# Hi and lo parts of each prepared weight stored in turn, element by element, in an encoder kernel on one core

## The chip, the core and the metric

The kernel runs on one core of one Trainium2 chip. The time is device time in microseconds, from one launch. Every change is judged against the kernel before; here smaller is better. Times of several executions are given as their median.

## The reference

Two layers of a bidirectional encoder over 256 tokens of 1024 channels, all in float32. What matters here is that nearly all the work is products with weights:

```
for i in range(2):
    h = x + 0.5 * swiglu(rms_norm(x, norm_ffn1[i]), w_ffn1_in[i], w_ffn1_out[i])     # 1024 -> 2 x 2816 -> 1024
    u = rms_norm(h, norm_mix[i])
    q, k, v, c, g = split(u @ w_in[i])                                               # 512, 128, 128, 1024, 2048
    y_attn = window_attention(norm(q), norm(k), v, sink[i], rel_bias) @ w_attn_out[i]
    y_conv = silu(layer_norm(depthwise_conv(glu(c)))) @ w_conv_out[i]
    h = h + (sigmoid(g)[:, :1024] * y_attn + sigmoid(g)[:, 1024:] * y_conv) @ w_o[i]
    h = h + 0.5 * swiglu(rms_norm(h, norm_ffn2[i]), w_ffn2_in[i], w_ffn2_out[i])
    x = h + (p[i] @ w_pe_proj[i]) * sigmoid(rms_norm(h, norm_pe[i]) @ w_pe_gate[i])
```

## The kernel before

**Products in three matmuls.** A float32 weight is cut into two parts of the type float32r: `hi`, the weight rounded to that type, and `lo`, what is left over. Activations are cut the same way. A product is then hi·hi + hi·lo + lo·hi, which `mm3` (lines 309 to 317) issues as three matmuls for each of the 128-row pieces of the contraction. In `mm3` the weight is the stationary operand (128 columns, loaded into TensorE's array by a load of its own ahead of each matmul) and the activations, 256 tokens, are the moving operand. Two stages do it the other way round: keys and values (`half`, lines 669 to 678) and queries (`part`, lines 713 to 722) have the activations as the stationary and the weights as the moving operand. `w_attn_out` and `w_conv_out` are used as plain float32 straight from the loaded buffer (line 852).

**Weights as one long list.** `Weights` holds a list of units (transfers of up to 1 MB from memory into one of 4 `raw` buffers, issued on SyncE's queue, line 76) and a list of specs (what one `get` hands out: k pieces of n columns). `get` (line 124) prepares LOOK = 6 specs ahead of the one that it hands out. `prep_upto` (line 80) prepares one: ScalarE copies the raw weight into `w_hi` with rounding (line 100), then VectorE writes raw minus hi into `w_lo` (line 101). The pool `w_pool` has 7 buffers of `w_hi` and 7 of `w_lo`, 4 KB in each partition, so that a copy into a buffer waits for the last matmul of the spec seven places earlier.

**Stages and order.** For each layer: 22 steps of `gate_up` (tiles `ps_gu`), 8 of `down` (`ps_fo`), the mixer (`ps_c` convolution input, `ps_kv`, `ps_q`, `ps_g` gates, attention between them, `ps_ao`, `ps_co`, then `ps_wo`), the second feed-forward part, and the per-layer embedding (`ps_pp`, `ps_pe`). TensorE runs in the program's order. The order on the other engines comes from a planner that works with priorities; `ws.later` hooks put attention steps between the weight products by hand. The convolution's taps run on VectorE in the background of the mixer (line 612).

**Where tiles lie.** Small tiles that nothing reads (`edge` of 96 bytes, `gap0`, `gap1` of 64) stand between the pools. In the program as built, every prepared weight tile starts at a multiple of 128 bytes in its partition and every activation tile that `mm3` reads starts 64 bytes after one.

Of the kernel before, what the change touches and what calls it, by code (L numbers as in the profile page):

```python
# [10 lines left out]
F32R = mybir.dt.float32r  # L11
# [4 lines left out]
P = 128  # L16
T = 256
D = 1024
KD = D // P
# [4 lines left out]
QD = 512  # L24
CD = 512
KC = CD // P
# [15 lines left out]
class Weights:  # L42
# [13 lines left out]
        self.units.append((k, n, sources))  # L56
        return len(self.units) - 1

    def spec(self, k, n, pieces):

        self.specs.append((k, n, pieces, False))

    def raw_spec(self, unit, k, c0, n):
        self.specs.append((k, n, [(unit, 0, c0, 0, n)], True))

    def limit(self):
        held = [p[0] for s in self.specs[self.next_get : self.next_prep] if s[3] for p in s[2]]
        return min(held) + RAW_BUFS - 1 if held else len(self.units) - 1

    def load_upto(self, u):  # L70
# [9 lines left out]
    def prep_upto(self, i):  # L80
        nc = self.nc
        while self.next_prep <= min(i, len(self.specs) - 1):
            k, n, pieces, as_is = self.specs[self.next_prep]
            for u, *_ in pieces:
                self.load_upto(u + RAW_BUFS - 2)
                if u >= self.next_load:
                    return
            if as_is:
                ((u, k0, s0, _, w),) = pieces
                self.ready[self.next_prep] = self.raw[u][:, k0 : k0 + k, s0 : s0 + w]  # L90
                self.next_prep += 1
                continue
            hi = self.w_pool.tile([P, KD * P], F32R, name="w_hi")
            lo = self.w_pool.tile([P, KD * P], F32R, name="w_lo")
            hv = hi[:, : k * n].rearrange("p (k n) -> p k n", n=n)
            lv = lo[:, : k * n].rearrange("p (k n) -> p k n", n=n)
            for u, k0, s0, d0, w in pieces:
                src = self.raw[u][:, k0 : k0 + k, s0 : s0 + w]
                parts = (
                    nc.scalar.copy(out=hv[:, :, d0 : d0 + w], in_=src),  # L100
                    nc.vector.tensor_tensor(  # L101
                        out=lv[:, :, d0 : d0 + w],
                        in0=src,
                        in1=hv[:, :, d0 : d0 + w].bitcast(F32),
                        op=ALU.subtract,
                    ),
                )
                if self.pin:
                    for ins in parts:
                        self.pin(ins)  # L110
                    self.pin = None
            self.ready[self.next_prep] = (hv, lv)
            self.next_prep += 1
# [25 lines left out]
def encoder_kernel(ctx: ExitStack, tc: tile.TileContext, a: dict, out: bass.AP):  # L139
# [30 lines left out]
    for i in range(4):  # L170
        s = slice(i * 256, (i + 1) * 256)
# [32 lines left out]
    ws = Weights(tc, raw_pool, w_pool)  # L204
# [4 lines left out]
    def cols_unit(w, k, c0, n):  # L209
        return ws.unit(k, n, [(whole, w[: k * P, c0 : c0 + n].rearrange("(k p) n -> p k n", p=P))])  # L210
# [25 lines left out]
    def mix_specs(l):  # L236
        w = a["w_in"][l]
        c0 = QD + 2 * P

        def conv_specs(j, n):  # L240
            uv = cols_unit(w, KD, c0 + j * P, n * P)
            ug = cols_unit(w, KD, c0 + CD + j * P, n * P)
            for c in range(n):
                ws.spec(KD, P, [(uv, 0, c * P, 0, P)])
                ws.spec(KD, P, [(ug, 0, c * P, 0, P)])

        conv_specs(0, 2)
        ukv = cols_unit(w, KD, QD, 256)
        for i in range(2):
            ws.spec(KC, 256, [(ukv, i * KC, 0, 0, 256)])  # L250
        for i in range(2):
            uq = cols_unit(w[i * KC * P : (i + 1) * KC * P], KC, 0, QD)
            for k in range(0, KC, 2):
                ws.spec(2, QD, [(uq, k, 0, 0, QD)])
        conv_specs(2, 2)
        g0 = QD + 2 * P + 2 * CD
        for j in range(8):
            u = cols_unit(w, KD, g0 + j * 256, 256)
            for c in range(2):
                ws.spec(KD, P, [(u, 0, c * P, 0, P)])  # L260
        w = a["w_attn_out"][l]
        for j in range(2):
            src = w[:, j * 512 : (j + 1) * 512].rearrange("(v c p) n -> v p c n", v=2, p=HD)
            u = ws.unit(KC, 512, [
                (lambda v: v[0:HD], src[0]),
                (lambda v: v[HD : 2 * HD], src[1]),
            ])
            for c in range(2):
                ws.raw_spec(u, KC, c * 256, 256)
        w = a["w_conv_out"][l]  # L270
        for j in range(2):
            u = cols_unit(w, KC, j * 512, 512)
            for c in range(2):
                ws.raw_spec(u, KC, c * 256, 256)
        w = a["w_o"][l]
        for j in range(4):
            u = cols_unit(w, KD, j * 256, 256)
            for c in range(2):
                ws.spec(KD, P, [(u, 0, c * P, 0, P)])
# [10 lines left out]
    for l in range(L):  # L290
        ffn_specs(a["w_ffn1_in"][l], a["w_ffn1_out"][l], quick=l == 0)
        mix_specs(l)
        ffn_specs(a["w_ffn2_in"][l], a["w_ffn2_out"][l])
        pe_specs(l)
# [797 lines left out]
```

## Time and profile before

| what | value |
|---|---|
| time, median of 3 executions | 1156.94 us (1156.45 to 1158.47) |
| profiled execution: span, first to last instruction | 1155.8 us |
| TensorE busy with matmuls (PE) | 1136.7 us, 98% |
| TensorE busy with loads of the stationary operand (PEld) | 1100.9 us, 95% |
| VectorE (DVE) | 812.1 us, 70% |
| ScalarE (ACT) | 610.4 us, 53% |
| read from memory | 200.53 MB, mean 174 GB/s over the span |

The span is the only time that the profiled execution has; it lies 1.1 us under the median of the executions without a profile. PE and PEld are two rows of one engine: the load for the next matmul runs while the present one streams, so both can be busy all the time. The matmuls' recorded durations overlap (each ends after the next has begun), so the pace of TensorE is read from the starts of successive matmuls, not from durations.

### The profile page before, as it was taken

What the parts mean: (1) busy time and instruction counts of PE and PEld (TensorE: products, weight loads), DVE (VectorE), ACT (ScalarE), POOL (GpSimd) and SP (SyncE); (2) the same over time, 40 slices, a digit from 0 to 9 for tenths busy, and PEclk for the clock granted to TensorE, in tenths of its full rate; (3) what the DMA queues carried; (4) which work ended last, traced back from release to release, by engine and by line L of the source; (5) the groups of instructions that cost most, each with busy time, mean ns of one, the idle gap of its engine ahead of it and who ended that gap; (6) DMA issues with size and microseconds to landing.
All of it is one profiled execution on the core that took longest, in us unless ns stands there. A gap on an engine that the chain in (4) does not pass through costs nothing.

```text
span 1155.8 us, 21813 instructions
## 1 busy us (share of the span) xinstructions
PE 1136.7 (98%) x9082; PEld 1100.9 (95%) x9082; DVE 812.1 (70%) x1214; ACT 610.4 (53%) x1029; POOL 88.8 (8%) x123
## 2 busy tenths in 40 slices
PE   7999999999989999999999999999999999999998
PEld 7999999998879999999999999999987899999997
DVE  5866656798767766656886666669986686666564
ACT  6644444676346544444664444457753564444443
POOL 3000001211002000001110000113000010000110
PEclk9999999999999999999999999999999999999999
DMA  8866556545074565546556464566522664644541
GB/s 256 265 236 213 170 176 208 182 149 138 8 254 157 187 215 168 179 166 219 188 177 204 162 207 156 171 218 197 143 77 65 227 228 152 214 163 149 200 147 37
DMA packets 195695, 203.00 MB, mean 176 GB/s; under 512 B 3731, under 2 KB 188899, under 8 KB 195596
## 3 DMA queue, kind: packets, MB, share of 16 engines
q1 hardware_dynamic: 195564, 201.60, 52.9%
q8 instruction: 71, 1.16, 0.4%
q14 instruction: 28, 0.23, 0.1%
q10 hardware_dynamic: 32, 0.01, 0.0%
HBM read 200.53 MB, written 1.06 MB: 174 GB/s over the span
## 4 chain that ended last, share of the span: by engine, by line
PE 95%; DMA 2%; DVE 2%; ACT 1%; issue 0%; SPq 0%; ACTq 0%; DVEq 0%
PE ps_gu L317 14%; PE ps_gu L315 14%; PE ps_gu L316 14%; PE ps_fo L315 7%; PE ps_fo L317 7%; PE ps_fo L316 7%; PE ps_g L315 3%; PE ps_g L317 3%; PE ps_g L316 3%; PE ps_ao L852 2%; DMA raw<-in_w_o_dram 2%; PE ps_s L760 1%; PE ps_wo L316 1%; PE ps_c L315 1%; PE ps_pe L317 1%; PE ps_c L317 1%
## 5 line engine op out<-in xcount | busy, mean ns | idle before, releaser
L101 DVE TENSOR_TENSOR w_lo<-raw,w_hi 128x1024 fp32r<-128x1024 f32 (+1 forms) x368 | 441.6, 1204 | 227.8 <-ACT w_hi L100 225.9
L100 ACT CAST w_hi<-raw 128x1024 fp32r<-128x1024 f32 (+1 forms) x368 | 377.8, 1032 | 411.6 <-PE ps_gu L316 207.5
L315 PE MATMUL ps_fo<-h_hi,w_hi 128*128 128x256 f32 x704 | 196.1, 279 | 0.0
L316 PE MATMUL ps_fo<-h_lo,w_hi 128*128 128x256 f32 x704 | 195.9, 279 | 0.0
L317 PE MATMUL ps_fo<-h_hi,w_lo 128*128 128x256 f32 x704 | 195.9, 279 | 0.0
L317 PEld LDWEIGHTS ps_fo<-h_hi,w_lo 128*128 128x128 f32 x704 | 131.8, 188 | 0.0
L315 PEld LDWEIGHTS ps_fo<-h_hi,w_hi 128*128 128x128 f32 x704 | 131.8, 188 | 0.0
L316 PEld LDWEIGHTS ps_fo<-h_lo,w_hi 128*128 128x128 f32 x704 | 131.7, 187 | 0.0
L404 POOL TENSOR_TENSOR sq_acc<-sq_acc,sq 128x256 f32<-128x256 f32 x56 | 56.9, 1015 | 887.0 <-ACT sq L403 886.5
L315 PE MATMUL ps_gu<-x0h,w_hi 128*128 128x256 f32 x352 | 99.4, 282 | 2.0 <-ACT x L460 2.0
L612 DVE SCALAR_TENSOR_TENSOR y<-cpad,cw,y 128x256 f32<-128x256 f32 x240 | 101.2, 477 | 0.1
L317 PE MATMUL ps_gu<-x0h,w_lo 128*128 128x256 f32 x352 | 99.4, 282 | 0.2 <-DVE w_lo L101 0.2
L316 PE MATMUL ps_gu<-x0l,w_hi 128*128 128x256 f32 x352 | 98.9, 281 | 0.0
L315 PE MATMUL ps_gu<-xf0h,w_hi 128*128 128x256 f32 x352 | 98.6, 280 | 0.0
L315 PE MATMUL ps_gu<-xf1h,w_hi 128*128 128x256 f32 x352 | 98.6, 280 | 0.0
L316 PE MATMUL ps_gu<-xn0l,w_hi 128*128 128x256 f32 x352 | 98.5, 280 | 0.0
L315 PE MATMUL ps_gu<-xn0h,w_hi 128*128 128x256 f32 x352 | 98.4, 280 | 0.0
L316 PE MATMUL ps_gu<-xf0l,w_hi 128*128 128x256 f32 x352 | 98.4, 280 | 0.0
L316 PE MATMUL ps_gu<-xf1l,w_hi 128*128 128x256 f32 x352 | 98.4, 280 | 0.0
L317 PE MATMUL ps_gu<-xf0h,w_lo 128*128 128x256 f32 x352 | 98.3, 279 | 0.0
L317 PE MATMUL ps_gu<-xf1h,w_lo 128*128 128x256 f32 x352 | 98.3, 279 | 0.0
L317 PE MATMUL ps_gu<-xn0h,w_lo 128*128 128x256 f32 x352 | 98.2, 279 | 0.0
(225 smaller groups left out, 2677.8 us busy)
## 6 DMA issues: line engine op xcount, KB each, us to landing
raw<-in_w_ffn_in_dram SPq DMA_DIRECT2D x86, 1024.0 KB
raw<-in_w_in_dram SPq DMA_DIRECT2D x30, 1024.0 KB
raw<-in_w_ffn_out_dram SPq DMA_DIRECT2D x32, 896.0 KB
raw<-in_w_ffn_out_dram SPq DMA_DIRECT2D x16, 1024.0 KB
raw<-in_w_o_dram SPq DMA_DIRECT2D x8, 1024.0 KB
raw<-in_w_pe_gate_dram SPq DMA_DIRECT2D x8, 1024.0 KB
raw<-in_w_attn_out_dram SPq DMA_DIRECT2D x8, 512.0 KB
raw<-in_w_conv_out_dram SPq DMA_DIRECT2D x4, 1024.0 KB
```

The lines of the kernel that those rows point to most:

```text
L100: nc.scalar.copy(out=hv[:, :, d0 : d0 + w], in_=src),
L101: nc.vector.tensor_tensor(out=lv[:, :, d0 : d0 + w], in0=src, in1=hv[:, :, d0 : d0 + w].bitcast(F32), op=ALU.subtract,),
L315: nc.tensor.matmul(ps, wh[:, k0 + k, cols], xh[:, kx, :], start=f, stop=False)
L316: nc.tensor.matmul(ps, wh[:, k0 + k, cols], xl[:, kx, :], start=False, stop=False)
L317: nc.tensor.matmul(ps, wl[:, k0 + k, cols], xh[:, kx, :], start=False, stop=e)
L404: nc.gpsimd.tensor_tensor(out=self.acc, in0=self.acc, in1=sq, op=ALU.add)
L612: nc.vector.scalar_tensor_tensor(out=y[:, i, :], in0=src, scalar=w, in1=y[:, i, :], op0=ALU.mult, op1=ALU.add)
L760: nc.tensor.matmul(ps[:, c, :], qT[v * HD : (v + 1) * HD, c, qb * P : (qb + 1) * P], kT[v * HD : (v + 1) * HD, :], start=True, stop=True,)
L852: nc.tensor.matmul(ps[:, c * T : (c + 1) * T], w[:, k, c * P : (c + 1) * P], x[:, k, :], start=k == 0, stop=k == KC - 1,)
```

## The change

Hi and lo of a spec now share one tile `w` of twice the size. Where the weight will be the stationary operand, element 2j of a row holds hi and element 2j + 1 holds lo, so each is read and written with a step of two elements. Where it will be the moving operand (keys and values, queries), the spec is marked `moving`, and hi and lo keep two halves of the tile, each without gaps. Numbers of instructions and of transfers, the arithmetic and the buffers' total size stay the same.

```diff
-    def spec(self, k, n, pieces):
-        self.specs.append((k, n, pieces, False))
+    def spec(self, k, n, pieces, moving=False):
+        self.specs.append((k, n, pieces, "moving" if moving else "stationary"))
...
-            hi = self.w_pool.tile([P, KD * P], F32R, name="w_hi")
-            lo = self.w_pool.tile([P, KD * P], F32R, name="w_lo")
-            hv = hi[:, : k * n].rearrange("p (k n) -> p k n", n=n)
-            lv = lo[:, : k * n].rearrange("p (k n) -> p k n", n=n)
+            w = self.w_pool.tile([P, 2 * KD * P], F32R, name="w")
+            if kind == "moving":
+                hv, lv = (w[:, i * KD * P :][:, : k * n].rearrange("p (k n) -> p k n", n=n) for i in range(2))
+            else:
+                both = w[:, : 2 * k * n].rearrange("p (k n s) -> p k n s", n=n, s=2)
+                hv, lv = both[:, :, :, 0], both[:, :, :, 1]
...
-            ws.spec(KC, 256, [(ukv, i * KC, 0, 0, 256)])
+            ws.spec(KC, 256, [(ukv, i * KC, 0, 0, 256)], moving=True)
...
-                ws.spec(2, QD, [(uq, k, 0, 0, QD)])
+                ws.spec(2, QD, [(uq, k, 0, 0, QD)], moving=True)
```

More of the change, by code (lines that the diff above doesn't have):

```diff
@@ L57, in unit @@
         return len(self.units) - 1
-    def spec(self, k, n, pieces):
-        self.specs.append((k, n, pieces, False))
+    def spec(self, k, n, pieces, moving=False):
+        self.specs.append((k, n, pieces, "moving" if moving else "stationary"))
     def raw_spec(self, unit, k, c0, n):
-        self.specs.append((k, n, [(unit, 0, c0, 0, n)], True))
+        self.specs.append((k, n, [(unit, 0, c0, 0, n)], "raw"))
     def limit(self):
-        held = [p[0] for s in self.specs[self.next_get : self.next_prep] if s[3] for p in s[2]]
+        held = [p[0] for s in self.specs[self.next_get : self.next_prep] if s[3] == "raw" for p in s[2]]
         return min(held) + RAW_BUFS - 1 if held else len(self.units) - 1
@@ L82, in prep_upto @@
         while self.next_prep <= min(i, len(self.specs) - 1):
-            k, n, pieces, as_is = self.specs[self.next_prep]
+            k, n, pieces, kind = self.specs[self.next_prep]
             for u, *_ in pieces:
@@ L87, in prep_upto @@
                     return
-            if as_is:
+            if kind == "raw":
                 ((u, k0, s0, _, w),) = pieces
```

## The prediction

> **What bounds the kernel now.** I read the page's engine rows and its chain first, then the stretches of the span, and then the starts of single matmuls. The page:
>
> ```profile
> span 1155.8 us, 21813 instructions
> ...
> PE 1136.7 (98%) x9082; PEld 1100.9 (95%) x9082; DVE 812.1 (70%) x1214; ACT 610.4 (53%) x1029; POOL 88.8 (8%) x123
> ...
> PE 95%; DMA 2%; DVE 2%; ACT 1%; issue 0%; SPq 0%; ACTq 0%; DVEq 0%
> ```
>
> TensorE is 95% of the chain that ends last. The waits say that it hardly ever waits for a prepared weight: the only such row is the first below, once in the run, while ScalarE waits for the matmuls to free its buffers (second row), so preparation runs a full seven buffers ahead.
>
> ```profile
> PE ps_gu L317 <- DVE w_lo L101: 0.2, 1, 0.2
> ACT w_hi L100 <- PE ps_gu L316: 207.5, 141, 1.9
> ```
>
> So the time is the number of matmuls times their pace. A long stretch of the second feed-forward part (columns: stretch, its length, then busy time and count of PE, PEld, DVE, ACT):
>
> ```profile
> 385.00:580.00 195.00, 195.00 (x1656) 194.95 (x1656) 132.09 (x172) 99.31 (x147) 10.14 (x11) 1.00 0.56 187
> ```
>
> 195.00 / 1656 = 0.1178 us per matmul of 256 moving columns. Is that the least it can be? The order of time, start and duration first:
>
> ```profile
> 13.77 0.41 PE L315 MATMUL ps_gu<-x0h,w_hi 128*128 128x256 f32 x1
> ...
> 14.62 0.41 PE L316 MATMUL ps_gu<-x0l,w_hi 128*128 128x256 f32 x1
> ...
> 214.01 0.28 PE L676 MATMUL ps_kv<-w_hi,xm0h 128*128 128x256 f32 x1
> ...
> 219.35 0.28 PE L678 MATMUL ps_kv<-w_hi,xm0l 128*128 128x256 f32 x1
> 219.69 0.40 PE L721 MATMUL ps_q<-w_lo,xm0h 128*128 128x512 f32 x1
> ...
> 226.00 0.39 PE L721 MATMUL ps_q<-w_lo,xm0h 128*128 128x512 f32 x1
> ...
> 312.63 0.60 PE L874 MATMUL ps_yt<-ident,y 128*128 128x128 f32 x4
> 313.06 0.60 PE L852 MATMUL ps_ao<-o,raw 128*128 128x256 f32 x2
> ```
>
> Keys and values have the same sizes, 48 matmuls with 256 moving columns and a load of 128, but weight and activations exchanged: (219.35 - 214.01) / 47 = 0.1136. Transposes, each with a load of 128 columns, follow one another every (313.06 - 312.63) / 4 = 0.1075. So 0.1178 holds about 0.010 us that is neither streaming nor loading at its best. It is constant through the run and does not depend on what the other engines do, so I take it to arise inside TensorE's own reads: the load for the next matmul and the moving stream read SBUF at once, and 0.1136 against 0.1178 shows that which operand is read on which side matters.
>
> **The change, part by part.**
>
> *The stationary operand read with a step of two.* A matmul streams 256 x 4 = 1024 bytes of each partition while the load beside it runs over 128 x 4 = 512. After the change the load runs over 128 x 8 = 1024 bytes in the same time: both streams walk through the addresses at the same speed, and by the layout they start 64 bytes apart modulo 128. If they disturb each other where they meet, then today one overtakes the other again and again; at equal speed they stay apart. No row shows a stationary operand with a step, so the price has two ends from rows: 0.1136 (keys and values, the other fp32r rows of this size) and 0.1075 (the transposes' row). Neither row is nearer in kind: the first has the same types, the second shows what a load and a short stream need at least. I take the middle, 0.1106, a gain of 0.0072 for each matmul. How many there are:
>
> ```profile
> L315 PE MATMUL ps_fo<-h_hi,w_hi 128*128 128x256 f32 x704 | 196.1, 279 | 0.0
> L315 PE MATMUL ps_gu<-x0h,w_hi 128*128 128x256 f32 x352 | 99.4, 282 | 2.0 <-ACT x L460 2.0
> L315 PE MATMUL ps_g<-xm0h,w_hi 128*128 128x256 f32 x128 | 36.8, 287 | 0.0
> L315 PE MATMUL ps_pe<-xe_h,w_hi 128*128 128x256 f32 x128 | 36.5, 286 | 0.0
> L315 PE MATMUL ps_wo<-ym_h,w_hi 128*128 128x256 f32 x128 | 35.1, 282 | 0.5 <-ACT ym_h L448 0.5
> L315 PE MATMUL ps_c<-xm1h,w_hi 128*128 128x256 f32 x64 | 18.1, 282 | 0.0
> L315 PE MATMUL ps_pp<-pT_h,w_hi 128*128 128x256 f32 x32 | 8.9, 280 | 0.0
> ```
>
> Three lines each: 3 x 704, 12 x 352 (four feed-forward parts), 6 x 128 (two layers), 3 x 128, 3 x 128, 6 x 64, 3 x 32, together 8352. Some 17 at the start run at (14.62 - 13.77) / 4 = 0.2125 and gain nothing. 8335 x 0.0072 = 60.0 us less. Ends: 8335 x 0.0042 = 35 and 8335 x 0.0103 = 86.
>
> The Trainium skill, SBUF — State Buffer, section Specifications (TRN2), gives lines of 16 bytes of which at least two accesses must hit each for full bandwidth. By it a step of two 4-byte elements, two hits in a line, is just allowed, and the load would not get longer; no run here shows it yet. The skill's TensorE: Matmul & The Clock Gate, section "Step-by-step: what each phase is for", speaks against my gain: two independent read ports, and a load that takes no bandwidth from the running matmul. By that the sum would be 1156; the 0.1136 beside 0.1178 does not fit it well, and I weigh it as the first rival.
>
> *Writing hi and lo with a step.*
>
> ```profile
> L101 DVE TENSOR_TENSOR w_lo<-raw,w_hi 128x1024 fp32r<-128x1024 f32 (+1 forms) x368 | 441.6, 1204 | 227.8 <-ACT w_hi L100 225.9
> L100 ACT CAST w_hi<-raw 128x1024 fp32r<-128x1024 f32 (+1 forms) x368 | 377.8, 1032 | 411.6 <-PE ps_gu L316 207.5
> ```
>
> Of 368 each, 12 (keys, values, queries) keep their form. A copy and a subtraction take 1.03 and 1.20 us for a tile whose 24 matmuls last 24 x 0.1106 = 2.65 us, so nothing shows on the path unless a row grows: the cover is 2.65 - 1.20 = 1.45 us less what else VectorE does in that time. Bounds: nothing, or twice as long. I take nothing: both rows go at 1.0 to 1.2 ns for each of 1024 elements, and no row shows a cost of a gap. Twice as long would bring VectorE to 812 + 441.6 x 356 / 368 = 1239 us busy, over the span; it is a rival below.
>
> *One tile for both parts.* If a reader of hi now also waits for the writer of lo, the first product waits; elsewhere preparation is ahead. The first matmul starts at 11.12 and the first with lo at 12.11:
>
> ```profile
> 11.12 0.58 PE L315 MATMUL ps_gu<-x0h,w_hi 128*128 128x256 f32 x1 [2.04 <-ACT x L460]
> ...
> 12.11 0.58 PE L317 MATMUL ps_gu<-x0h,w_lo 128*128 128x256 f32 x1 [0.19 <-DVE w_lo L101]
> ```
>
> Between 0 and 0.99 us; I take the two matmuls that would move behind it, 2 x 0.2125 = 0.4. A buffer becomes free one matmul later (line 317, not 316), 0.12 us out of a lead of seven tiles: nothing. Queues and transfers are unchanged, on SyncE's queue too.
>
> *What is late next.* Faster products need weights faster: the stretch above read 187 GB/s, times 0.1178 / 0.1106 is 199, and the page's second slice has 265:
>
> ```profile
> GB/s 256 265 236 213 170 176 208 182 149 138 8 254 157 187 215 168 179 166 219 188 177 204 162 207 156 171 218 197 143 77 65 227 228 152 214 163 149 200 147 37
> ```
>
> In the mixer VectorE's taps must finish before the layer norm; there 3 x 64 + 3 x 128 = 576 products arrive 576 x 0.0072 = 4.1 us sooner per layer, and VectorE waits there for products long enough to follow: 12.7 us in two layers for the gates alone.
>
> ```profile
> DVE g L833 <- PE ps_g L317: 12.7, 8, 2.3
> ```
>
> *Sum:* 1155.8 - 60.0 + 0.4 = 1096.2 us of span. The median lies 1.1 above the span, so 1097 us.
>
> **The rivals.**
>
> *The pace stays.* Queries speak for it: (226.00 - 219.69) / 27 = 0.2337 for 512 columns, twice 0.1169, though the load beside each covers only half of the stream. If the moving stream alone sets 0.1178, the change does nothing: 1157 us (1155 to 1158). Against it stand keys and values at 0.1136, whose moving stream has the same length.
>
> *The streams meet more often, slower.* The load now touches twice the addresses in the same time. If what counts is how many places are touched, or if the load walks backwards, the excess of 0.0103 over 0.1075 grows up to twofold: 0.1281, 86 us more, up to 1243. It decides from a pace of 0.1181 on. For it: the excess exists only with two streams at full speed. Against it: at equal speed a pair that has slipped apart once stays so.
>
> *The load takes twice as long.* A load of 128 columns takes about as long as a stream of 256, as the transposes' 0.1075 bounds it. If each step of two costs double, the pace is 0.215 and the time 1157 + 8335 x 0.097 = 1966. Nothing in the trace speaks for it but that loads have no slack.
>
> *Writing takes twice as long.* VectorE bounds at 1239 us and more, some 1260.
>
> **How the numbers follow.** A faster pace 0.58, the same pace 0.15, more meetings 0.17, slow loads 0.05, slow writing 0.05. The likeliest gives 1097, with its own range 1071 to 1122 from the two ends. Cases of both signs hold much of the chance, so the range goes up to the lower part of the third case: 1075 to 1200 leaves out the two last, the upper half of the third and a little below. About 0.2%, 2.3 us or 0.0003 us of pace, is what a measurement of this kernel can tell from no change: faster 0.58, same 0.15, slower 0.27.
>
> **What would show it.** Right: in the same stretch of feed-forward work the count of matmuls per microsecond gives 0.108 to 0.114, keys, values and queries keep 0.1136 and 0.2337, the plain float32 products (line 852) keep theirs, and the preparing rows keep 1.03 and 1.20 us. The first step is wrong if the pace stays at 0.1178 or passes it; the second if L100 or L101 grows and TensorE waits on `w`; the third if TensorE has more than one wait on a weight at the start.

## The result and the profile after

| | before | after |
|---|---|---|
| median | 1156.7 us (1155.83 to 1158.47, 4 executions) | 1176.05 us (1175.6 to 1176.45, 4 executions) |
| ratio, 95% interval | | 1.0165 [1.015, 1.0179] |
| span of the profiled execution | 1155.8 us | 1174.7 us |

The change makes the kernel 1.65% slower, 18.9 us of span. A gain of 60 us was forecast. 1176 us lies inside the stated range of 1075 to 1200, but only because that range was drawn wide enough for cases of both signs. The engine rows, the chain and the rows of preparing and loading in the page of the changed kernel (copy and subtraction are now lines 102 and 103, the three products lines 317 to 319):

```profile
span 1174.7 us, 21713 instructions
...
PE 1156.5 (98%) x9082; PEld 1121.5 (95%) x9082; DVE 814.2 (69%) x1214; ACT 640.5 (55%) x1029; POOL 78.1 (7%) x123
...
PE 95%; DMA 2%; DVE 2%; ACT 1%; issue 0%; ACTq 0%; DVEq 0%
...
L102 ACT CAST w<-raw 128x1024 fp32r<-128x1024 f32 (+1 forms) x368 | 411.1, 1123 | 408.6 <-PE ps_gu L319 208.1
L103 DVE TENSOR_TENSOR w<-raw,w 128x1024 fp32r<-128x1024 f32 (+1 forms) x368 | 442.3, 1205 | 257.6 <-ACT w L102 257.3
...
L317 PEld LDWEIGHTS ps_fo<-h_hi,w 128*128 128x128 f32 x704 | 139.1, 198 | 0.0
```

TensorE is still 98% busy and 95% of the chain, with the same 9082 matmuls. (The counts of all engines are as before; the 100 fewer instructions of the first line, 21713 for 21813, are of kinds that do not count as busy.) VectorE's row is as before. ScalarE's copy has grown from 1032 to 1123 ns, but it still waits 208.1 us for matmuls to free its buffers (207.5 before): preparation is still ahead. So the 19 us are in the pace. The same stretch as before, busy time and count of PE, PEld, DVE, ACT, POOL:

```profile
385.00:580.00 195.00, 195.00 (x1626) 194.95 (x1625) 127.46 (x163) 102.05 (x140) 8.20 (x9) 1.00 0.55 184
```

In 195 us stand 1626 matmuls, where 1656 stood: 0.1199 us each for 0.1178. Such a count takes in one to three matmuls that began before the stretch, so the paces below are read from the starts of single matmuls. In the long stretches of feed-forward work these are 120.0 ns after and 117.78 before, and 8335 x 2.22 ns = 18.5 us, nearly the whole loss. The load's own row has grown too; the line below is of the page before (188 ns), the one of after is above (198):

```profile
L315 PEld LDWEIGHTS ps_fo<-h_hi,w_hi 128*128 128x128 f32 x704 | 131.8, 188 | 0.0
```

Where the weight is the moving operand nothing changed. Keys and values of the changed kernel, first and last of 47 in a row (the planner put the first of the 48 some 7 us earlier, as in every version with one tile):

```profile
218.33 0.28 PE L679 MATMUL ps_kv<-w,xm0h 128*128 128x256 f32 x1
...
223.56 0.28 PE L680 MATMUL ps_kv<-w,xm0l 128*128 128x256 f32 x1
```

(223.56 - 218.33) / 46 = 0.1137, as the 0.1136 of before.

### The profile page after: what moved, and what is told of

Its sections match the earlier page's. It is cut to its first block, busy times and chain, and to the rows that moved or that the text cites. A ratio compares the mean times of both kernels' runs of the same rounds, so it can differ in the third digit from the quotient of the medians.

```text
span 1174.7 us, 21713 instructions
## 1 busy us (share of the span) xinstructions
PE 1156.5 (98%) x9082; PEld 1121.5 (95%) x9082; DVE 814.2 (69%) x1214; ACT 640.5 (55%) x1029; POOL 78.1 (7%) x123
## 4 chain that ended last, share of the span: by engine, by line
PE 95%; DMA 2%; DVE 2%; ACT 1%; issue 0%; ACTq 0%; DVEq 0%
PE ps_gu L319 14%; PE ps_gu L317 14%; PE ps_gu L318 14%; PE ps_fo L319 7%; PE ps_fo L318 7%; PE ps_fo L317 7%; PE ps_g L317 3%; PE ps_g L319 3%; PE ps_g L318 3%; PE ps_ao L854 2%; DMA raw<-in_w_o_dram 2%; PE ps_s L762 1%; PE ps_wo L318 1%; PE ps_c L317 1%; PE ps_c L319 1%; PE ps_c L318 1%
## 5 line engine op out<-in xcount | busy, mean ns | idle before, releaser
L102 ACT CAST w<-raw 128x1024 fp32r<-128x1024 f32 (+1 forms) x368 | 411.1, 1123 | 408.6 <-PE ps_gu L319 208.1
L103 DVE TENSOR_TENSOR w<-raw,w 128x1024 fp32r<-128x1024 f32 (+1 forms) x368 | 442.3, 1205 | 257.6 <-ACT w L102 257.3
L318 PE MATMUL ps_fo<-h_lo,w 128*128 128x256 f32 x704 | 199.1, 283 | 0.0
L319 PE MATMUL ps_fo<-h_hi,w 128*128 128x256 f32 x704 | 199.1, 283 | 0.0
L317 PE MATMUL ps_fo<-h_hi,w 128*128 128x256 f32 x704 | 198.6, 283 | 0.0
L318 PEld LDWEIGHTS ps_fo<-h_lo,w 128*128 128x128 f32 x704 | 139.4, 198 | 0.0
L319 PEld LDWEIGHTS ps_fo<-h_hi,w 128*128 128x128 f32 x704 | 139.4, 198 | 0.0
L317 PEld LDWEIGHTS ps_fo<-h_hi,w 128*128 128x128 f32 x704 | 139.1, 198 | 0.0
L317 PE MATMUL ps_gu<-x0h,w 128*128 128x256 f32 x352 | 101.4, 288 | 2.1 <-ACT x L462 2.1
L319 PE MATMUL ps_gu<-x0h,w 128*128 128x256 f32 x352 | 100.9, 287 | 0.2 <-DVE w L103 0.2
L317 PE MATMUL ps_gu<-xf0h,w 128*128 128x256 f32 x352 | 99.9, 284 | 0.0
L317 PE MATMUL ps_gu<-xf1h,w 128*128 128x256 f32 x352 | 99.9, 284 | 0.0
L317 PE MATMUL ps_gu<-xn0h,w 128*128 128x256 f32 x352 | 99.8, 284 | 0.0
L319 PE MATMUL ps_gu<-xn0h,w 128*128 128x256 f32 x352 | 99.6, 283 | 0.0
L319 PE MATMUL ps_gu<-xf0h,w 128*128 128x256 f32 x352 | 99.6, 283 | 0.0
L319 PE MATMUL ps_gu<-xf1h,w 128*128 128x256 f32 x352 | 99.6, 283 | 0.0
```

What stands on the lines that cost most here:

```text
L103: nc.vector.tensor_tensor(out=lv[:, :, d0 : d0 + w], in0=src, in1=hv[:, :, d0 : d0 + w].bitcast(F32), op=ALU.subtract,),
L317: nc.tensor.matmul(ps, wh[:, k0 + k, cols], xh[:, kx, :], start=f, stop=False)
L318: nc.tensor.matmul(ps, wh[:, k0 + k, cols], xl[:, kx, :], start=False, stop=False)
L319: nc.tensor.matmul(ps, wl[:, k0 + k, cols], xh[:, kx, :], start=False, stop=e)
```

## The experiments

Three suspects at the start: the read, a load with a step of two that disturbs the moving stream more; the write with a step, or the sharing of a tile; and the starts of the two operands, so that another layout would still give the gain forecast. Executions of one kernel spread by several us (1148.48 to 1159.65 in ten of the first run below), so runs with a single execution, which are most of them, are judged by their paces first.

**The three parts of the change, one at a time.** First one tile, with hi and lo in two halves without gaps:

```diff
-                both = w[:, : 2 * k * n].rearrange("p (k n s) -> p k n s", n=n, s=2)
-                hv, lv = both[:, :, :, 0], both[:, :, :, 1]
+                hv, lv = (w[:, i * KD * P :][:, : k * n].rearrange("p (k n) -> p k n", n=n) for i in range(2))
```

> Hi and lo share one tile, but every weight keeps two halves without gaps, so only the sharing of the tile is left of the change. Theory 1 (the load of the stationary operand itself gets longer when it reads with a step of two) and theory 2 (the load and the moving stream meet more often): 1157 us, pace 0.1178 us for each matmul, ScalarE's copy 1.03 us. Theory 3 (sharing the tile delays the weights): 1176 us.

1157.16 us (10 executions), ratio 0.9994 [0.9976, 1.0013], and in the same stretch:

```profile
385.00:580.00 195.00, 195.00 (x1657) 194.94 (x1656) 132.20 (x172) 98.98 (x146) 10.14 (x11) 1.00 0.56 187
```

1657 matmuls, where the kernel before has 1656. Sharing the tile costs nothing that shows.

Then writing without gaps and reading with a step of two. What the matmuls read is then not the weights, so the output is another; instructions and sizes are those of the changed kernel.

```diff
-                hv, lv = both[:, :, :, 0], both[:, :, :, 1]
+                hv, lv = [w[:, i * k * n : (i + 1) * k * n].rearrange("p (k n) -> p k n", n=n) for i in range(2)]
...  # copy and subtraction write hv, lv
+            if kind == "stationary":
+                hv, lv = both[:, :, :, 0], both[:, :, :, 1]
             self.ready[self.next_prep] = (hv, lv)
```

> Weights are written without gaps and read by TensorE with a step of two elements (so the products mix hi and lo of neighbouring columns: the values are not the reference's). Theories 1 and 2: 1176 us, pace 0.120, copy 1.03 us. If the strided writing costs the time: 1157 us, pace 0.1178.

1175.0 us (one execution), span 1173.2, and in the same stretch:

```profile
385.00:580.00 195.00, 195.00 (x1626) 194.95 (x1625) 127.42 (x162) 97.20 (x140) 8.68 (x9) 1.00 0.55 184
```

and in the page its copy:

```profile
L102 ACT CAST w<-raw 128x1024 fp32r<-128x1024 f32 (+1 forms) x368 | 378.7, 1034 | 431.0 <-PE ps_gu L321 219.5
```

1626 matmuls, as in the changed kernel, while the copy is back at 1034 ns. Reading alone brings the pace of the changed kernel and, to about 1 us, its time.

The mirror of it, writing with the step (and, as before, other numbers to the matmuls), reading without:

```diff
+                halves = [w[:, i * k * n : (i + 1) * k * n].rearrange("p (k n) -> p k n", n=n) for i in range(2)]
...  # copy and subtraction write every second element
+            if kind == "stationary":
+                hv, lv = halves
```

> Weights are written with a step of two elements and read by TensorE without gaps (the values are not the reference's). Theories 1 and 2: 1157 us, pace 0.1178, copy 1.12 us. If the strided writing costs the time: 1176 us, pace 0.120.

1152.95 us (one execution), span 1151.2. Two stretches of this run, then its copy from the page:

```profile
60.00:130.00 70.00, 70.00 (x620) 70.00 (x619) 49.29 (x66) 36.63 (x52) 0.00 (x0) 1.00 0.59 200
...
385.00:580.00 195.00, 195.00 (x1657) 194.95 (x1656) 132.56 (x175) 104.31 (x152) 12.00 (x14) 1.00 0.55 184
```

```profile
L103 ACT CAST w<-raw 128x1024 fp32r<-128x1024 f32 (+1 forms) x368 | 406.4, 1110 | 392.0 <-PE ps_gu L322 198.8
```

Writing costs nothing on the path, though the copy takes 1110 ns. And there is something that no theory had: between 60 and 130 us stand 620 matmuls, 0.1129 us each, where the kernel before has 597 (0.1173):

```profile
60.00:130.00 70.00, 70.00 (x597) 70.00 (x596) 47.33 (x64) 33.87 (x50) 0.00 (x0) 1.00 0.60 203
```

By the starts the step is 113.33 ns from about 54 to 202 us, and 117.78 in the other feed-forward work. Some 1300 matmuls x 4.45 ns = 5.8 us, near the 4.6 by which this span is shorter than the 1155.8 of the kernel before. So matmuls of one form have two steady paces in one run. The faster one begins right behind another product (`ps_rb`) and ends at the statistics' products of the mixer (`ps_stat`). The same products stand there in the kernel before, without a change of pace, so such an interruption can switch it but need not.

**A table of paces.** Not the encoder: 48 matmuls in a row of each kind, with starts of stationary and moving operand, the step, and the sizes varied.

```python
lhs = w[:, sb : sb + c * step].rearrange("p (n s) -> p n s", s=step)[:, :, 0]   # step 1: w[:, sb : sb + c]
nc.tensor.matmul(ps[:c, :n], lhs, x[:, mb : mb + n], start=r == 0, stop=r == reps - 1)
```

> No encoder: only 48 matmuls of the same type for each of 34 cases, by the step of the stationary operand (1, 2, 3, 4, 8 elements), by where the two operands start modulo 128 bytes, by moving columns (256, 512) and stationary columns (128, 64); the output is not the reference's. Theory 1: step two gives 0.120 at every pair of starts, step one 0.1178 or less; with 512 moving columns both steps give the same 0.233; with 64 stationary columns the load is no longer the bound and both steps give the same, 0.108 to 0.114; steps of 3, 4 and 8 are longer than 0.120. Theory 2: step two varies by more than 0.004 with the distance between the starts, and some distance is faster than step one. For step one with the weight at 64 and the activations at 0, as for keys and values, 0.1136 if the place modulo 128 is what sets those apart, 0.1178 if not.

Rows of four groups by tile, the last with its load (`t` step, `s` and `m` starts of stationary and moving operand modulo 128 bytes; durations min/median/max in ns, then first and last start in us):

```profile
L96 PE MATMUL t1s0m64n256c128x<-x,w x48: 276/276/278, 36.9 to 42.2; 128*128 128x256 f32 x48
L96 PE MATMUL t1s0m0n256c128x<-x,w x48: 281/283/283, 48.0 to 53.6; 128*128 128x256 f32 x48
L96 PE MATMUL t2s0m64n256c128x<-x,w x48: 280/283/285, 93.5 to 99.1; 128*128 128x256 f32 x48
L96 PE MATMUL t4s0m64n256c128x<-x,w x48: 388/394/403, 167.7 to 178.7; 128*128 128x256 f32 x48
L96 PEld LDWEIGHTS t4s0m64n256c128x<-x,w x48: 317/329/329, 167.6 to 178.5; 128*128 128x128 f32 x48
```

Paces from the starts, in ns (here and below the mean step from the ninth start of a group on). Apart from VectorE's copy of each result out of PSUM (the memory in which TensorE leaves results) nothing else runs beside these matmuls, so the differences need no other engine:

| starts, stationary/moving | step 1 | step 2 |
|---|---|---|
| 0/64 | 113.3 | 120.0 |
| 64/0 | 117.8 | 120.1 |
| 0/0 and 64/64 | 120.0 | 120.0 |
| 0/32, 0/96 | 116.6, 119.9 | 121.0, 120.0 |
| 0/16, 16/0 | 116.6, 118.4 | 118.3, 120.0 |
| 0/64, 64/0 with 512 moving columns | 228.9, 233.3 | 233.3, 230.0 |
| 0/64, 64/0 with 64 stationary columns | 116.7, 113.3 | 118.9, 115.6 |

At 256 x 128 a step of two has 118.3 to 121 at every pair of starts; a step of one has anything from 113.3 to 120. Neither theory comes out whole: a step of one is not always 117.8 or less, the rows with 512 and with 64 columns are not the same for both steps, and at no pair of starts is a step of two the faster. At 64/0, the arrangement of keys and values, the pace was 117.8, and 113.3 stood at the reverse. Steps of three, four and eight (starts 0/64) take 174.7, 233.2 and 240.0 ns, with load records of 263, 329 and 337 ns against 188: there the load is taken to be the bound. The Trainium skill, SBUF — State Buffer, section Specifications (TRN2), asks for at least two accesses to each line of 16 bytes for full bandwidth, and has each cross to a new line pay a penalty. 4-byte elements four or more apart are one to a line; twice the time for them is an estimate worked out from that row. 233.2 ns at a step of four and 240.0 at eight fit it; 120.0 at two, where full bandwidth would be left, is above 113.3 at the same starts, and whether that is the penalty for crossing, twice as often as at a step of one, no run here shows. The Trainium skill's TensorE: Matmul & The Clock Gate, section "Step-by-step: what each phase is for", has the load take no SBUF read bandwidth from the running matmul. A step of one that runs at 113.3 with starts 0/64 and at 120.0 with 0/0 does not fit that, and the measurement decides.

**Does what stands ahead set the pace?** 36 matmuls of each layout, behind nothing, a plain fp32 matmul, transposes, an idle time, or a matmul of another width; all of it twice.

> A table of paces, not the encoder: 84 groups of 36 matmuls of 256 moving and 128 stationary columns, in two turns; ahead of each group stands nothing, a plain fp32 matmul, four transposes, an idle time, or a matmul of 512, 320 or 64 moving columns. Six layouts: stationary step 1 with starts 0/64, 64/0, 0/0, 0/32 (bytes modulo 128, stationary/moving), step 2 with 0/64 and 0/0. Theory A (a step of one has several steady paces, and what stands ahead of a group can move it from one to another; a step of two always loses the full 6.67 ns): step 1 at 0/64 is found at both 113.3 and 117.8 ns, step 2 in all its groups at 120 within 1 ns. Theory B (the pace follows from the starts alone): step 1 at 0/64 is 113.3 in every group, 64/0 is 117.8 in every group, 0/0 is 120. Theory C (a step of two is caught in a bad state that the right interruption frees): some step 2 groups at 113.3 to 117.8.

The group behind nothing at 0/64 with a step of one, first turn and second:

```profile
L99 PE MATMUL noneat1s0m64x<-x,w x36: 279/279/283, 36.1 to 40.2; 128*128 128x256 f32 x36
L99 PE MATMUL nonebt1s0m64x<-x,w x36: 276/276/280, 221.0 to 225.0; 128*128 128x256 f32 x36
```

(40.2 - 36.1) / 35 = 0.117 us and (225.0 - 221.0) / 35 = 0.114; from the starts 117.78 and 113.33 ns. These are the same matmuls on the same addresses. Step 1 at 64/0 was found at both paces too: the starts alone don't decide between them. But 0/0 ran at 120.0 or 120.1 in all its groups, so the starts do count. Behind a matmul of 64 moving columns 0/64 ran at 113.33 in both turns. Step 2 ran at 120.0 to 121.5, a little over what theory A allowed. (Behind the idle time each group has a longer step in its midst, up to 240 ns, so its mean is left out.) No interruption tried here frees a step of two, so theory C falls for the kinds tried.

**Other starts in the encoder.** Moving operands moved by 64 bytes, so that both begin at 0, in the kernel before and in the changed one:

```diff
-        nc.gpsimd.memset(gap.tile([P, 16], F32, name="gap"), 0.0)
+        nc.gpsimd.memset(gap.tile([P, 32 if gap is gap0 else 16], F32, name="gap"), 0.0)
```

> The kernel before with 16 more floats in the first gap, so that moving operands and weights both start at 0 modulo 128 bytes (0 and 64 in the kernel before). Theory A and B (the pace comes from how loads and moving reads meet, and equal starts lose 6.67 ns at a step of one too): the pace goes from 117.75 to 120.0 ns, 8335 matmuls x 2.25 = +19 us, 1176 us without any step in the layout. Rival (the loss of the changed kernel is the longer load alone): equal starts do nothing, 1157 us.

> The changed kernel with 16 more floats in the first gap, so that moving operands and weights both start at 0 modulo 128 bytes. Theory A (a step of two loses the full 6.67 ns at any start): 120.0 ns, 1176 us, as the changed kernel. Rival (the step changed only which starts suit each other, and a shift of 64 bytes gives it back): 113.3 to 117.8 ns, 1120 to 1157 us.

The kernel before goes to 1165.67 us, the changed one to 1182.28, one execution each. The kernel before as it was had 1151.81 in its only execution beside these runs. One stretch of each, the kernel before with equal starts first:

```profile
390.00:590.00 200.00, 200.00 (x1687) 199.95 (x1686) 134.82 (x179) 102.76 (x153) 12.69 (x14) 1.00 0.54 180
```

```profile
390.00:590.00 200.00, 200.00 (x1653) 199.95 (x1652) 131.37 (x169) 105.64 (x146) 9.51 (x10) 1.00 0.55 182
```

200 / 1687 = 0.1186 and 200 / 1653 = 0.1210. Without any step, equal starts cost the kernel before 9 us against its usual 1156.7, or 14 against 1151.81; 19 were expected, but the pace is 118.7 ns in most of three of the four feed-forward parts and 120.0 only in the other. In both kernels the keys and values, whose two operands then also start at 0, go from 113.6 to 118.6 ns. So a loss of this kind needs no wider reach of the load: here each load of the kernel before still reads 512 bytes without gaps. And a shift does not rescue the step of two: this one execution is 6 us slower than expected.

Weights at 64 and moving operands at 0, the arrangement of keys and values:

```diff
-    edge = const.tile([P, 24], F32, name="edge")
+    edge = const.tile([P, 40], F32, name="edge")
```

> The kernel before with 16 more floats ahead of its pools, so that weights start at 64 and moving operands at 0 modulo 128 bytes (exchanged). Theory B (starts alone; keys and values, with stationary at 64 and moving at 0, run at 113.33 in the kernel before): 113.33 ns for the 8335, 8335 x 4.4 = -37 us, 1120 us, and keys and values go to 117.75. By the table of paces (64/0 ran at 117.77): 117.77, 1157 us. Theory A (both paces open, and what stands ahead decides): anything between 1120 and 1157 us, with a pace that changes at interruptions.

1152.17 us (one execution). From about 54 to 202 us it runs at 113.33 (620 matmuls between 60 and 130 us, as in the run that wrote with a step), and in the later feed-forward work at 117.78. Keys and values stay at 113.6 with their starts exchanged, where theory B had 117.75. Both paces are open here too; the starts alone don't settle it.

**Can the better pace be had on purpose?** A table again: four transposes, then four groups of 24 matmuls with a step of one, between them nothing or one matmul of another size.

> A table of paces, not the encoder: groups of 24 matmuls of 256 moving and 128 stationary columns with a step of one, starts 0/64 and 64/0; ahead of each set stand four transposes, and between its four groups nothing, or one matmul of another size (16 to 512 moving columns, or 32 or 64 stationary columns). Theory A (one of several steady paces is kept until something shifts the loads against the moving reads): each set begins at 117.78 ns after the transposes, stays there with nothing between, and some of the odd sizes move the groups behind them to 113.33. Rival (the pace is set by the starts and by slow drift, not by what stands between): no kind changes the pace of the groups behind it in a way that is the same in both turns.

With nothing between, each pace is kept through all four groups. At 0/64 none of the eleven kinds brought a group from 117.8 to 113.3; the groups with 32 stationary columns between ran at 113.33, but from before the first of these on. At 64/0 seven of the kinds switch it to and fro, the same way in both turns; one of 192 moving columns left 113.33 behind it six times in six. Three attempts in the encoder, the first planned on the table before (113.33 behind 64 moving columns) at the same time as this one:

```diff
+        calls[0] += 1
+        if first and calls[0] % 2 == 0:
+            nc.tensor.matmul(ps[:, :64], wh[:, k0, cols], xh[:, x_k0, :64], start=True, stop=True)
```

> The kernel before, with one more matmul of 64 moving columns ahead of every second product of a tile (144 more, whose result the product behind it overwrites). Theory A (such a matmul moved groups at starts 0/64 to 113.33 ns in the table): most of the 8335 at 113.33, -37 us, and 144 matmuls at 0.12 to 0.24 = +17 to +35 us: 1137 to 1157 us. Rival (it does not move the pace): 117.75, +17 to +35 us, 1173 to 1191 us.

1169.61 us (one execution): the pace stays at 117.78, and the 144 added matmuls cost (1169.61 - 1151.81) / 144 = 0.124 us each, or 0.090 against the usual 1156.7 of the kernel before. The rival has the pace, and the time lies just under its range. Then with 192 columns (`xh[:, x_k0, :192]`, `calls[0] % 4 == 1` or `% 12 == 1`) and the exchanged starts:

> The kernel before with weights at 64 and moving operands at 0 modulo 128 bytes, and 78 more matmuls of 192 moving columns, one ahead of every fourth first product of a tile (the product behind it overwrites what they write). Theory A (at starts 64/0 both paces are steady, and such a matmul left the groups behind it at 113.33 ns in all six cases of the table): about 8300 matmuls x 4.4 = -37 us, 78 x 0.09 = +7 us: 1122 to 1130 us beside 1152 to 1157. Rival (in the kernel something pushes the pace back within a tile or two, or the table's pattern does not carry over): 117.75 ns in most stretches, 1157 to 1164 us.

> As the run before, with a third of the added matmuls (26, one ahead of every twelfth first product). Theory A: the pace holds between them, -37 + 2 us: 1118 to 1125 us. Rival (the pace is pushed back between them): between this and 1160 us, with 113.33 ns only in a stretch behind each.

1163.13 us, ratio 1.006 [1.0043, 1.0076], and 1157.15 us, ratio 1.0013 [0.9998, 1.0027]. The first of them in the stretch used above:

```profile
390.00:590.00 200.00, 200.00 (x1700) 199.95 (x1700) 134.88 (x178) 102.77 (x153) 12.89 (x14) 1.00 0.55 180
```

1700 matmuls in 200 us, as without any help (1697 in the kernel before). 113.33 shows only from 42 to 47 us, behind one of the added matmuls, from 55 to 57 and for 8 steps near 345. The second, with 28 added matmuls by the count, has it from 42 to 47 us alone. (Keys and values, which keep their pace, are left out.) The rival holds: what the table showed does not carry over, and neither version beats the kernel before.

**Load length or interplay?** Moving columns, stationary columns and step varied apart, at four pairs of starts and twice.

> A table of paces, not the encoder: groups of 24 matmuls, at four pairs of starts and in two turns, with steps of 1 and 2 and moving columns from 256 to 512, stationary columns from 32 to 128, and a few steps of 3 and 4. Theory L (the load with a step of two is a stream of its own that lasts about 117 ns, half of the 233 that a step of four measured, and so it, not the moving stream of 113.3, bounds the pace at 256 columns): with moving columns 272 to 512, or with 96 or fewer stationary columns, the mean over the starts is the same for steps 1 and 2 within 1 ns; a step of four with 64 columns paces as a step of two with 128. Theory M (each load takes up to 6.67 ns from the moving stream, a step of two always the whole): step 2 stays 2 to 6 ns above step 1 at every number of moving columns, each at the floor of n/256 x 113.33 ns plus 6.67.

Means of the eight groups, in ns; the floor is 113.33 for each 256 moving columns:

| moving x stationary columns | floor | step 1 | step 2 |
|---|---|---|---|
| 256 x 128 | 113.3 | 117.8 | 120.5 |
| 272 x 128 | 120.4 | 125.9 | 126.2 |
| 288 x 128 | 127.5 | 132.8 | 133.3 |
| 320 x 128 | 141.7 | 146.7 | 147.9 |
| 384 x 128 | 170.0 | 174.6 | 175.5 |
| 512 x 128 | 226.7 | 230.6 | 233.0 |
| 256 x 96 | 113.3 | 116.9 | 118.9 |
| 256 x 64 | 113.3 | 117.0 | 117.7 |
| 256 x 32 | 113.3 | 114.3 | 116.6 |

Two pairs of rows at starts 0/0, first with 512 moving columns, then with 32 stationary ones:

```profile
L98 PE MATMUL uat1n512c128s0m0x<-x,w x24: 389/389/397, 289.6 to 294.8; 128*128 128x512 f32 x24
L98 PE MATMUL uat2n512c128s0m0x<-x,w x24: 392/394/394, 295.0 to 300.4; 128*128 128x512 f32 x24
L98 PE MATMUL uat1n256c32s0m0x<-x,w x24: 276/276/280, 323.2 to 325.9; 128*32 128x256 f32 x24
L98 PE MATMUL uat2n256c32s0m0x<-x,w x24: 276/280/283, 326.0 to 328.7; 128*32 128x256 f32 x24
```

(294.8 - 289.6) / 23 = 0.226 us and (300.4 - 295.0) / 23 = 0.235; from the starts 226.7 and 233.3. A stream of 512 columns is twice as long as one of 256, yet the step of two costs 6.7 ns there. With 32 stationary columns, a quarter of the load, it costs 3.9 (113.3 and 117.2). These are starts where the two differ most. At 64/0 with 512 columns both ran at 233 in the first turn, and the step of two was the faster in the second and in the first table (230 for 233); with 32 columns both ran at 113.33 at 64/0 in the first turn, and at about 117 at 0/32.

By the means, theory L holds to 1 ns in four of the eight rows that it speaks of (272, 288, 384 and 64 columns) and misses in the others by 1.2 to 2.4, so the load as a bound of its own falls as the general reason. At a step of four it does look like one: 64 columns ran at 119.3 with load records of 193 ns, nearly the 188 of 128 columns at a step of one, while a step of two with 128 columns has only 195. Theory M falls in its numbers: the difference between the steps is 0.3 to 2.7, not 2 to 6, because a step of one loses 3.6 to 5.5 on the mean as well (1.0 with 32 columns). What stands: with 128 stationary columns, at the stream lengths tried, a step of two lies 5.5 to 7.2 ns above the floor on the mean, and a step of one 3.9 to 5.5, in some groups nothing. Three orders of the operands beside this one (every matmul other operands, all the same, and hi, hi, lo as in `mm3`) gave means of 117.2 to 117.5 and 120.2 to 120.3 at 256 x 128.

## Why the prediction was wrong

*The stationary operand read with a step of two: the step that failed.* The prediction priced each matmul at 0.1106 us, a gain of 7.2 ns, on the ground that two streams at equal speed stay apart. The encoder went to 0.1200, a loss of 2.2 ns, and the run that only reads with the step shows that this is where the loss lies. At every pair of starts tried, a step of two with 256 x 128 columns ran at 118.3 ns or more, mostly at 120, so "at equal speed they stay apart" gave nothing. The rival "the streams meet more often" had the direction and the place right, reading alone; its size was wrong. It let the excess grow by up to 10.3 ns, to 0.1281; it grew by 2.2 in the encoder, and no group of that size in the tables went over 121.8. The point from which that rival decides, 0.1181, was passed. Whether the streams do meet more often is not shown by this.

*The two ends of that price.* 0.1075 from the transposes was no floor for these matmuls: no group of 256 fp32r columns came under 113.33, even with a quarter of the stationary columns. So the excess that any version here got rid of was 4.4 ns, not 10.3, and the middle, 0.1106, was under every pace measured: 8335 x 4.4 = 37 us at best. Keys and values were rightly taken as a hint that reads matter: with other starts they went from 113.6 to 118.6. That "which operand is read on which side" sets it was wrong: with the weights as the stationary operand as before, both paces occurred.

*The pace stays* is refuted by 2.2 ns on each matmul, and by starts that move the pace.

*Writing hi and lo: nothing.* Right for the time: the run that only writes with the step keeps the pace. For the rows it was right for VectorE (1204 and 1205 ns) and wrong for ScalarE (1032 and 1123, 9% more), which the cover hid as told.

*One tile: 0.4 us.* It came to nothing. In the changed kernel the first product with lo starts 1.00 us after the first with hi, 0.99 before, with the same short wait for the subtraction (0.2 us); the first with hi does not wait for it. The experiment with one tile alone gives 0.9994, too coarse to tell 0.4 us.

*Loads or writing twice as long*: neither. A pace about twice as long comes at a step of four (233.2 ns), not at two.

*What is late next* had nothing to test: the products came slower, not faster.

What is not settled: why the pace lies up to some 7 ns above its floor, how a step of two in the load comes to raise it, and what picks one of the two paces for a step of one. The tables give bounds for these, no explanation.

## What to carry to other kernels

A stationary operand read with a step of two elements of 4 bytes was not free here, although the load ran beside another matmul's stream: price it at the upper end of what the same matmuls show with a step of one (here 120 ns), not at a layout that has not been seen. Before taking the gap between two rows as a gain to be had, find the floor with rows of the same type and width; a transpose was not one. Two runs that differ by some 5 us can differ in the pace of one long stretch alone: read the pace by stretch before giving a small difference to an edit.

## What was not expected of the hardware

- One stream of matmuls, on the same addresses, has two steady paces: 117.78 and 113.33 ns for the same group in two turns of one table. In the encoder one of them held for some 150 us, and the two runs with such a stretch were some 5 us shorter (span 1151.2 and 1150.4 against 1155.8). Single executions near 1149 us exist of the kernel before too (1149.04, without a trace); whether this is their reason is not shown.
- The starts of stationary and moving operand modulo 128 bytes move the pace: at a step of one 0/0 ran at 120.0 or 120.1 ns in all groups counted, 0/64 at 113.3 or 117.8, and keys and values went from 113.6 to 118.6 when both began at 0.
- ScalarE's copy grows by 8 to 9% when it writes every second element (1032 to 1110 and 1123 ns); VectorE's subtraction, which also reads such an operand, does not (1204 and 1205 ns).
- With loads of steps 3, 4 and 8 the pace is 174.7, 233.2 and 240.0 ns at 256 x 128 columns and starts 0/64: a step of eight costs little more than one of four.
